# The first modulation vectors of a hybrid layer on TensorE: fp32 weights that stand still and a two-column vector that moves, with their first loads ahead of the token loads

## The chip, the cores and the metric

The kernel runs on one core of a Trainium2 chip. The metric is the device time of one execution in microseconds (us); lower is better. A core has five engines that each work through their own instructions in order: TensorE (PE in the profile, with its weight loads on a row of their own, PEld), VectorE (DVE), ScalarE (ACT), GpSimd (POOL) and SyncE (SP), which here issues nearly all of the DMAs.

## The reference, cut to what matters

One layer of a diffusion backbone: 512 latent tokens and 256 context tokens of width 1024. Two conditioning vectors, one for the latent tokens and one for the context, go through a matrix of 1024 x 6144 and give six modulation vectors each. The first two of the six (shift and scale) are applied to the normalised tokens ahead of one wide input projection:

```python
mod_x = (silu(c) @ w_ada + b_ada).reshape(1, 6, 1, 1024)
mod_c = (silu(c_ctx) @ w_ada + b_ada).reshape(6, 1024)
hc = rms_norm(ctx, norm1_w) * (1.0 + mod_c[1]) + mod_c[0]
hx = rms_norm(x, norm1_w) * (1.0 + mod_x[:, 1]) + mod_x[:, 0]
zs = hn @ w_in   # for hn = hc and hx: q, k, v and gates of two token mixers
```

Two recurrent mixers (a gated delta rule and an mLSTM), an output projection, a gated residual and a gated MLP with a 3x3 convolution follow. The output is compared in fp32, so the kernel keeps fp32 accuracy throughout.

## The kernel before

**Products.** A large product of fp32 accuracy is made as three products of a rounded type (fp32r): both operands are split into hi (a cast, ACT, line 104) and lo (fp32 minus hi, line 105, on DVE or POOL), and `mm3` (lines 112 to 116) adds hi*hi, hi*lo and lo*hi. In all of these the tokens are the moving operand and 128 columns of the weight matrix the standing one.

**First stage, about the first 80 us.** `streams` (line 345) loads six blocks of 128 tokens (two of context, four latent), squares and sums them on ACT (line 320), scales them (DVE, 322), turns them over on PE (327, eight transposes a block) and copies the turned halves to `xT` (ACT 330, DVE 332). Then a loop over k = 0 to 7 (128 channels each) needs the modulation of these channels: `stream_mod` makes hi of the modulated tokens on ACT (341: `hx` for the 512 latent tokens, `hc` for the 256 of the context), the fp32 value on DVE (342) and lo (343: DVE for `hx`, POOL for `hc`). The products of step k are 12 matmuls: the gates' 128 columns (`ps_gc`, `ps_gx`) and the first head's key columns (`pc_k`, `px_k`), three of 256 and three of 512 moving columns for each. Beside them the first head's query columns (`px_q`, weight `wq0`, 24 matmuls of 512 columns) are taken up as their operands come. When the loop has ended, ACT evicts the gates (411, 412), PE turns them (`ps_gt`, 441), DVE and ACT make the decays, PE forms the running sums (`ps_gs`, 456) and turns them again (`ps_gr`, 480), DVE copies them (482), a DMA writes them out (`gd`) and others read them back as the masks of all heads (`Eg`). The inverse of the delta rule's first heads starts from these masks.

**The modulation of the first stage** is 16 blocks of 1024 x 128 of `w_ada`, 512 KB each: `uw` k, j for channel block k and shift or scale j. `ada_load` (224) issues their DMAs on SP; the tiles share one tag of 7 buffers (`XN`) with the six token blocks and the assembled gate weights. `ada_rows` (231) lets the vectors stand and the weights move: for 14 blocks the weight is split into hi `uh` (ACT, 243) and lo `ul` (DVE or POOL, 244), and 16 matmuls run with 4 standing columns (hi and lo of both vectors, `sch`) and 128 moving (247); two blocks (`UF`) run as plain fp32 (239). The result is 4 rows of 256, which ACT copies (249); `ada_cols` (253) turns them with two small transposes (256) and DVE adds bias and parts (258, 261, 262) to give `mod` and `modA`.

**What sets the order.** A scheduler at build time lays out each engine's queue from the program order and its own model of durations; nothing moves at run time. An ACT instruction that waits for its operand holds all ACT instructions behind it, and the same goes for PE's matmuls. SP's DMAs of the first stage stand in the order tokens, first weights, `wk0`, the `uw` blocks, then `wq0` (`w_cols`, line 110, through `load_split`).

Of the kernel before, what the change touches and what calls it, by code (L numbers as in the profile page):

```python
# [70 lines left out]
class Kern:  # L71
# [131 lines left out]
    def ada_first(self, xp):  # L203
        nc, I, cp = self.nc, self.I, self.cp
        th = xp.tile([P, 16], F32, tag="c_th", name="c_th")
        nc.scalar.activation(th, self.ccol, AF.Tanh, scale=0.5)
        sc0 = xp.tile([P, 16], F32, tag="sc0", name="sc0")
        nc.vector.scalar_tensor_tensor(sc0, th, 1.0, self.ccol, ALU.add, ALU.mult)
        self.sc = cp.tile([P, KC, 2], F32, tag="sc", name="sc")
        nc.vector.tensor_scalar(self.sc.rearrange("p k j -> p j k"), sc0.rearrange("p (j k) -> p j k", j=2), 0.5, None, ALU.mult)  # L210
        self.sch = xp.tile([P, KC, 4], F32R, tag="sch", name="sch")
        nc.vector.tensor_copy(self.sch[:, :, 0:2], self.sc)
        nc.vector.tensor_tensor(self.sch[:, :, 2:4], self.sc, self.sch[:, :, 0:2].bitcast(F32), ALU.subtract)
        self.sc4 = xp.tile([P, KC, 4], F32, tag="sc4", name="sc4")
        nc.vector.memset(self.sc4, 0.0)
        nc.vector.tensor_copy(self.sc4[:, :, 0:2], self.sc)
        self.bada4 = xp.tile([P, 16, 4], F32, tag="bada4", name="bada4")
        nc.vector.memset(self.bada4, 0.0)
        nc.vector.tensor_copy(self.bada4[:, :, 0:2], self.bada[:, 0:16].unsqueeze(2).broadcast_to([P, 16, 2]))
        self.mod = cp.tile([P, 16, 2], F32, tag="mod", name="mod")  # L220
        self.modA = cp.tile([P, KC, 2], F32, tag="modA", name="modA")
        self.modB = self.mod[:, 0:8, :]

    def ada_load(self, k, j, xp):

        w = xp.tile([P, KC, P], F32, tag="xn", name=f"uw{k}_{j}", bufs=XN)
        c0 = D * j + P * k
        self.anchor["d"] = self.nc.sync.dma_start(w, self.I["w_ada"][0][:, c0 : c0 + P].rearrange("(k p) c -> p k c", p=P))
        return w

    def ada_rows(self, k, ap):

        nc = self.nc
        ps = self.pt([P, 512], ("mg", "po")[k % 2], f"ps_ada{k}")
        for j in range(2):
            w = self.uw[2 * k + j]
            if (2 * k + j) in UF:
                for i in range(KC):
                    nc.tensor.matmul(ps[0:4, P * j : P * j + P], self.sc4[:, i, :], w[:, i, :], start=i == 0, stop=i == KC - 1)
                continue  # L240
            hi = ap.tile([P, KC, P], F32R, tag="uh", name=f"uh{k}_{j}", bufs=UH)
            lo = ap.tile([P, KC, P], F32R, tag="ul", name=f"ul{k}_{j}", bufs=UH)
            nc.scalar.copy(hi, w)
            (nc.vector, nc.gpsimd)[(2 * k + j) in UP].tensor_tensor(lo, w, hi.bitcast(F32), ALU.subtract)
            for i in range(KC):
                for p in (hi, lo):
                    nc.tensor.matmul(ps[0:4, P * j : P * j + P], self.sch[:, i, :], p[:, i, :], start=i == 0 and p is hi, stop=i == KC - 1 and p is lo)
        r = ap.tile([4, 2 * P], F32, tag="adr", name=f"adr{k}", bufs=2)
        nc.scalar.copy(r, ps[0:4, 0 : 2 * P])
        return ps, r  # L250

    def ada_cols(self, k, ps, r, ap):

        nc = self.nc
        for j in range(2):
            nc.tensor.transpose(ps[:, 256 + 4 * j : 260 + 4 * j], r[:, P * j : P * j + P], self.ident[0:4, 0:4])
        t = ap.tile([P, 2, 4], F32, tag="adt", name=f"adt{k}", bufs=2)
        nc.vector.tensor_tensor(t, ps[:, 256:264].rearrange("p (n j) -> p n j", j=4),
                                self.bada4[:, k : 16 : KC, :], ALU.add)
# [74 lines left out]
    def stream_mod(self, k, xp):  # L334
        nc = self.nc
        A, B = self.modA[:, k, :], self.modB[:, k, :]
        for (h, n0, n1, j, e) in ((self.hx, NCTX, NALL, 0, nc.vector), (self.hc, 0, NCTX, 1, nc.gpsimd)):
            hh, hl = h
            src = self.xT[:, k, n0:n1]
            t = xp.tile([P, n1 - n0], F32, tag=f"hl_t{j}", name="hl_t", bufs=2 - j)  # L340
            nc.scalar.activation(hh[:, k, :], src, AF.Identity, bias=B[:, j : j + 1], scale=A[:, j : j + 1])
            nc.vector.tensor_scalar(t, src, A[:, j : j + 1], B[:, j : j + 1], ALU.mult, ALU.add)
            e.tensor_tensor(hl[:, k, :], t, hh[:, k, :].bitcast(F32), ALU.subtract)

    def streams(self):

        with self.tc.tile_pool(name="xin", bufs=1) as xp, self.tc.tile_pool(name="ada", bufs=2) as ap:
            self.xT = xp.tile([P, KC, NALL], F32, tag="xT", name="xT")
            self.vectors(xp, 0)
            xs = [self.stream_load(c, xp) for c in range(2)]  # L350
            self.vectors(xp, 1)
            xs += [self.stream_load(c, xp) for c in range(2, 6)]
            self.ada_first(xp)
            self.uw = [self.ada_load(n // 2, n % 2, xp) for n in range(2)]
            wg = self.gates_weights(xp)
            self.sub_eng = self.nc.gpsimd
            wk = self.w_cols(self.I["w_in"][0], 1024, "wk0")
            self.uw += [self.ada_load(n // 2, n % 2, xp) for n in range(2, 16)]
            for c in range(6):
                self.stream_in(c, xs[c], xp)  # L360
            gx, gc = (self.pt([P, 512], "prep", f"ps_{n}") for n in ("gx", "gc"))
            kc, kx = (self.pt([P, 512], "sc", n) for n in ("pc_k0", "px_k0"))
            a = self.ada_rows(0, ap)
            for k in range(KC):
                self.ada_cols(k, *a, ap)
                self.stream_mod(k, xp)
                if k < KC - 1:
                    a = self.ada_rows(k + 1, ap)
                for (w, pc, px) in ((wg, gc, gx), (wk, kc, kx)):
                    for (ps, h, n) in ((pc, self.hc, NCTX), (px, self.hx, NT)):  # L370
                        self.mm3(ps[:, :n], w[0][:, k, :], w[1][:, k, :], h[0][:, k, :], h[1][:, k, :], k == 0, k == KC - 1)
            self.gates_rows(gx, gc)
            self.first = {"wk": wk, "pc_k0": kc[:, :NCTX], "px_k0": kx}


    def gates_weights(self, xp):

        nc, I, cp, tc = self.nc, self.I, self.cp, self.tc
        w = I["w_in"][0]
# [1132 lines left out]
```

## Time and profile before

| what | value |
|---|---|
| time before, median of 3 runs | 1418.37 us (1417.46 to 1422.01) |
| the profiled execution | 1419.17 us, of which the span is 1417.5 us |
| PE busy | 1323.7 us, 93% of the span |
| DVE, ACT, POOL busy | 919.3, 588.7, 492.9 us |
| DMA | 141.86 MB, 100 GB/s over the span |

A profile's span runs from the first instruction to the last; the execution's own time is 1.7 us more. A line of the timeline gives start, duration, engine, line, operation and tiles, and in brackets how long the engine had been idle and what ended that. A window's row gives for each engine the busy time and the number of instructions in that stretch, the granted clock of PE (1.00 is full, 0.50 half), the DMA share and GB/s. A matmul's duration holds the time to get through the array, so the pace of back-to-back matmuls is read from their starts.

### The profile page before, as it was taken

To read this page: it belongs to the slowest core of one execution; us is meant where nothing else is said; L and a number is where in the kernel's file an instruction comes from. 1 tells how busy PE (TensorE), PEld (TensorE's weight loads), DVE (VectorE), ACT (ScalarE), POOL (GpSimd) and SP (SyncE) were. 2 spreads that over 40 slices of the span, in tenths; PEclk is the share of its full clock that TensorE was granted. 3 is DMA by queue.
4 is the path that set the end of the run, shared out by engine and by line. 5 is a ranking of instruction groups with operands and counts; after the bars stand their busy time and mean duration, and the time that the engine had idled before them with its cause. 6 is when DMAs were issued, how large, how long until landed. Compare 5 with 4: busy or idle time off the path is not lost.

```text
span 1417.5 us, 24242 instructions
## 1 busy us (share of the span) xinstructions
PE 1323.7 (93%) x9436; PEld 1118.2 (79%) x9436; DVE 919.3 (65%) x1900; ACT 588.7 (42%) x1283; POOL 492.9 (35%) x591
## 2 busy tenths in 40 slices
PE   5988699999999999999999999879989999999997
PEld 4777588878887887889788887668887888888886
DVE  6648973748676683554655367455469879879933
ACT  6555554545556554333333345112234333333331
POOL 4425131130330303242500004770145555555552
PEclk9999799999999999999999999999999999999999
DMA  8533233231332323343422214765523233333321
GB/s 244 151 87 94 56 80 85 72 101 42 84 81 67 79 53 88 107 132 111 113 62 76 64 45 111 185 173 172 189 67 112 86 93 105 89 105 89 104 89 60
DMA packets 233234, 141.86 MB, mean 100 GB/s; under 512 B 32978, under 2 KB 215519, under 8 KB 233119
## 3 DMA queue, kind: packets, MB, share of 16 engines
q1 hardware_dynamic: 233118, 140.31, 35.6%
q8 instruction: 74, 1.21, 0.4%
q14 instruction: 42, 0.34, 0.1%
HBM read 134.47 MB, written 5.82 MB: 99 GB/s over the span
## 4 chain that ended last, share of the span: by engine, by line
PE 60%; DMA 12%; POOL 9%; DVE 9%; ACT 5%; issue 3%; SPq 0%; POOLq 0%; DVEq 0%; ACTq 0%
PE pu L115 11%; PE pu L116 5%; PE pd L115 5%; PE px_g L115 3%; PE pv L115 3%; PE pd L116 3%; POOL iv_t L758 2%; POOL gx L760 2%; DMA scr<-cdx 2%; PE po L115 2%; PE px_mo L115 2%; DMA oTg<-in_w_ada_dram 2%; PE py L115 2%; PE px_g L116 2%; PE px_q L115 2%
## 5 line engine op out<-in xcount | busy, mean ns | idle before, releaser
L1482 DVE SCALAR_TENSOR_TENSOR y<-pu,fw,y 128x441 f32<-128x441 f32 (+2 forms) x352 | 229.9, 690 | 39.7 <-ACT y L1473 34.1
L1031 POOL TENSOR_TENSOR mkw<-mkt,colB 128x768 f32<-128x768 f32 x8 | 12.8, 1607 | 137.5 <-PE mpc L1052 79.3
L139 POOL TENSOR_TENSOR kh<-pw_t,phalf 128x6 f32<-128x6 f32 x8 | 11.1, 1390 | 124.1 <-DVE pw_t L138 124.1
L895 DVE SCALAR_TENSOR_TENSOR X<-p,colA,vt 128x128 f32<-128x128 f32 x80 | 24.2, 345 | 33.2 <-PE p L891 33.1
L275 POOL TENSOR_TENSOR oTg<-oTg,sc 128x512 f32<-128x512 f32 x22 | 34.5, 1576 | 29.4 <-DMA oTg<-in_w_ada_dram 29.0
L777 POOL TENSOR_TENSOR qs<-qs,qT 128x512 f32<-128x512 f32 x16 | 20.7, 1294 | 62.4 <-DMA qs<-gd 55.8
L139 POOL TENSOR_TENSOR rs<-pw_t,mhalf 128x1 f32<-128x1 f32 x14 | 9.1, 653 | 92.9 <-DVE pw_t L138 92.9
L753 POOL MEMSET gx<- 96x16 f32 x8 | 1.0, 124 | 115.3 <-DMA gx<-scr 115.3
L911 PE MATMUL p<-v,kt 128*128 128x128 f32 x160 | 30.2, 305 | 10.6 <-ACT v L907 10.6
L758 POOL TENSOR_TENSOR iv_t<-gx 96x14 f32<-96x14 f32 (+6 forms) x112 | 37.0, 330 | 7.5
L907 ACT ACTIVATE v<-p,sc 128x128 f32<-128x128 f32 x80 | 25.4, 367 | 34.0 <-PE p L899 33.8
L1473 ACT ACTIVATE y<-pu,fw 128x512 f32<-128x512 f32 x44 | 30.0, 683 | 20.5 <-PE pu L116 12.6
L760 POOL TENSOR_TENSOR gx<-gx,iv_t 96x14 f32<-96x14 f32 (+6 forms) x112 | 34.0, 304 | 8.7
L911 PEld LDWEIGHTS p<-v,kt 128*128 128x128 f32 x160 | 23.3, 197 | 16.7 <-ACT v L907 14.8
L626 DVE SCALAR_TENSOR_TENSOR Eg<-Eg,colA,mask 128x128 f32<-128x128 f32 x96 | 32.7, 405 | 3.9 <-DMA Eg<-gd 3.8
L1424 POOL TENSOR_TENSOR al<-y,ah 128x512 fp32r<-128x512 f32 x22 | 28.7, 1304 | 14.8 <-ACT ah L1423 11.7
L1056 DVE SCALAR_TENSOR_TENSOR C<-C,ge,mpc 128x257 f32<-128x257 f32 x32 | 15.4, 480 | 28.0 <-PE mpc L1052 27.8
L918 DVE SCALAR_TENSOR_TENSOR S<-S,ge,p 128x128 f32<-128x128 f32 x64 | 19.3, 343 | 18.4 <-PE p L911 17.3
L277 POOL TENSOR_TENSOR oTg<-oTg 128x256 f32<-128x256 f32 (+1 forms) x44 | 30.0, 699 | 0.7
L1434 DVE TENSOR_TENSOR fd_t<-pd,m 128x512 f32<-128x512 f32 x8 | 5.3, 684 | 37.8 <-PE pd L116 37.8
L891 PE MATMUL p<-S,kT 128*128 128x128 f32 x160 | 29.7, 287 | 0.0
L924 ACT ACTIVATE v<-p,sc 128x128 f32<-128x128 f32 x64 | 23.0, 378 | 15.8 <-PE p L911 15.0
(1239 smaller groups left out, 4683.9 us busy)
## 6 DMA issues: line engine op xcount, KB each, us to landing
uw<-in_w_ada_dram SPq DMA_DIRECT2D x16, 512.0 KB
oTg<-in_w_ada_dram SPq DMA_DIRECT2D x32, 256.0 KB
Eg<-gd SPq DMA_DIRECT2D x16, 384.0 KB
gx<-in_w_ada_dram SPq DMA_DIRECT2D x23, 256.0 KB
qs<-gd SPq DMA_DIRECT2D x16, 256.0 KB
aw<-in_w_ada_dram SPq DMA_DIRECT2D x9, 256.0 KB
xn<-in_x_dram SPq DMA_DIRECT2D x4, 512.0 KB
Em<-r1d SPq DMA_DIRECT2D x8, 256.0 KB
```

Of the source, the lines that this page charges most:

```text
L115: for i in (mm(out, lh, rh, start=start, stop=False), mm(out, lh, rl, start=False, stop=False), mm(out, ll, rh, start=False, stop=stop)):
L116: mm(out, ll, rh, start=False, stop=stop)):
L275: eng.tensor_tensor(w, w, self.sc[:, 4 * i : 4 * i + 4, 0:1].broadcast_to([P, 4, P]), ALU.mult)
L277: eng.tensor_tensor(w[:, 0:m, :], w[:, 0:m, :], w[:, m : 2 * m, :], ALU.add)
L626: self.follow(nc.vector.scalar_tensor_tensor(E[:, c, :], E[:, c, :], self.colA[:, c, d, row : row + 1], self.mask[d], ALU.add, ALU.min), "v")
L758: eng.tensor_tensor(t, Bi[:, 0:j, j : j + 1].broadcast_to([8 * NB, j, n]), Bi[:, j : j + 1, j + 1 :].broadcast_to([8 * NB, j, n]), ALU.mult)
L760: g = eng.tensor_tensor(Bi[:, 0:j, j + 1 :], Bi[:, 0:j, j + 1 :], t, ALU.add)
L891: g = nc.tensor.matmul(p1[:, d, :], kT[:, c * P : c * P + P], S[d], start=True, stop=True)
L911: g = nc.tensor.matmul(p3[:, d, :], kt[:, c, :], v3[d], start=True, stop=True)
L1424: nc.gpsimd.tensor_tensor(al[:, j, :], ys[0], ah[:, j, :].bitcast(F32), ALU.subtract)
L1473: nc.scalar.activation(y, ps, AF.Copy, scale=tap(0, 0))
L1482: g = nc.vector.scalar_tensor_tensor(o, u3[:, r0 + dy : r1 + dy, c0 + dx : c1 + dx], tap(dy, dx), o, ALU.mult, ALU.add)
```

## The change

The vectors no longer stand; the weights do. `ada_mod(k)` takes the fp32 block as it was loaded, as the standing operand of 128 x 128, and lets the two columns of `sc` move: 8 matmuls a block, which PE runs as two fp32 passes each. The result comes out with channels on partitions, so the split of the weights, the 4-row copy, the transposes, `sch`, `sc4` and `bada4` all go, and one DVE addition of the bias stands in their place. The shared tag has 12 buffers in place of 7. `uw` 0,0 and 0,1 are loaded ahead of the context, `uw` 1,0 and 1,1 ahead of x. `ada_mod(0)` is issued ahead of the token work and `ada_mod(k+1)` ahead of `stream_mod(k)`. The lo of `hc` moves from POOL to DVE. The small gate vectors (`gb`, `en`) are loaded after the `uw` blocks in program order, in a function of their own, `gates_vectors`, which holds what stood at the end of `gates_weights`.

```diff
-UH = 3
-UF = (1, 7)
-UP = (0, 9, 13)
-XN = 7
+XN = 12
...
-    def ada_rows(self, k, ap):
+    def ada_mod(self, k):
...
-        ps = self.pt([P, 512], ("mg", "po")[k % 2], f"ps_ada{k}")
+        ps = self.pt([P, 2, 2], ("mg", "po")[k % 2], f"ps_ada{k}")
         for j in range(2):
             w = self.uw[2 * k + j]
-            nc.scalar.copy(hi, w)
-            (nc.vector, nc.gpsimd)[(2 * k + j) in UP].tensor_tensor(lo, w, hi.bitcast(F32), ALU.subtract)
             for i in range(KC):
-                for p in (hi, lo):
-                    nc.tensor.matmul(ps[0:4, P * j : P * j + P], self.sch[:, i, :], p[:, i, :], start=i == 0 and p is hi, stop=i == KC - 1 and p is lo)
-        nc.scalar.copy(r, ps[0:4, 0 : 2 * P])
...
-    def ada_cols(self, k, ps, r, ap):
...
+                nc.tensor.matmul(ps[:, j, :], w[:, i, :], self.sc[:, i, :], start=i == 0, stop=i == KC - 1)
         m = self.mod[:, k : 16 : KC, :]
-        nc.vector.tensor_tensor(m, t[:, :, 0:2], t[:, :, 2:4], ALU.add)
+        nc.vector.tensor_tensor(m, ps, self.bada[:, k : 16 : KC].unsqueeze(2).broadcast_to([P, 2, 2]), ALU.add)
         nc.vector.tensor_scalar(self.modA[:, k, :], self.mod[:, KC + k, :], 1.0, self.n1w[:, k : k + 1], ALU.add, ALU.mult)
...
-        for (h, n0, n1, j, e) in ((self.hx, NCTX, NALL, 0, nc.vector), (self.hc, 0, NCTX, 1, nc.gpsimd)):
+        for (h, n0, n1, j, e) in ((self.hx, NCTX, NALL, 0, nc.vector), (self.hc, 0, NCTX, 1, nc.vector)):
...
             self.vectors(xp, 0)
+            self.uw = [self.ada_load(0, j, xp) for j in range(2)]
             xs = [self.stream_load(c, xp) for c in range(2)]
             self.vectors(xp, 1)
+            self.uw += [self.ada_load(1, j, xp) for j in range(2)]
             xs += [self.stream_load(c, xp) for c in range(2, 6)]
             self.ada_first(xp)
-            self.uw = [self.ada_load(n // 2, n % 2, xp) for n in range(2)]
             wg = self.gates_weights(xp)
             self.sub_eng = self.nc.gpsimd
             wk = self.w_cols(self.I["w_in"][0], 1024, "wk0")
-            self.uw += [self.ada_load(n // 2, n % 2, xp) for n in range(2, 16)]
+            self.uw += [self.ada_load(n // 2, n % 2, xp) for n in range(4, 16)]
+            self.gates_vectors()
+            self.ada_mod(0)
             for c in range(6):
                 self.stream_in(c, xs[c], xp)
...
-            a = self.ada_rows(0, ap)
             for k in range(KC):
-                self.ada_cols(k, *a, ap)
+                if k < KC - 1:
+                    self.ada_mod(k + 1)
                 self.stream_mod(k, xp)
-                if k < KC - 1:
-                    a = self.ada_rows(k + 1, ap)
```

The order of the instructions is the scheduler's, so three places of it are shown. Lines of the changed kernel are some 3 to 33 lower (341 is 308 there, 104 is 101, 115 is 112). The name in brackets is a semaphore waited for; DMAHW is a DMA's landing.

The first place is ACT in the channel loop. Before, the cast of the query weights (`wq0h`) stands behind four steps of `hx` and `hc`, and ahead of the other four:

```order
L341 ACTIVATE hx_75<-xT,mod,modA 128x512 [waits DVE_49]
L341 ACTIVATE hc_81<-xT,mod,modA 128x256
L243 CAST uh_0_751<-uw_0_240 128x1024 [waits DMAHW4_49,PE_49,Pool_49]
L249 COPY adr_653<-ps_ada_612 4x256 [waits PE_49]
L243 CAST uh_1_771<-uw_1_242 128x1024 [waits DMAHW5_49,PE_49,Activation_49]
L104 CAST wq0h<-wq0r 128x1024 [waits DMAHW0_49]
L243 CAST uh_0_820<-uw_0_244 128x1024 [waits DMAHW6_49,DVE_49,PE_49]
L249 COPY adr_722<-ps_ada_681 4x256 [waits PE_49]
L341 ACTIVATE hx_75<-xT,mod,modA 128x512 [waits DVE_49]
L341 ACTIVATE hc_81<-xT,mod,modA 128x256
L243 CAST uh_1_840<-uw_1_246 128x1024 [waits DMAHW7_49,PE_49,Activation_49]
```

In the changed kernel it stands right behind the last copy of the turned tokens:

```order
L297 COPY xT<-ps_xt_0_323 128x4x128 [waits PE_49]
L297 COPY xT<-ps_xt_0_343 128x4x128 [waits PE_49]
L308 ACTIVATE hc_81<-xT,mod,modA 128x256 [waits DVE_49]
L297 COPY xT<-ps_xt_0_363 128x4x128 [waits PE_49]
L101 CAST wq0h<-wq0r 128x1024 [waits DMAHW0_49]
L308 ACTIVATE hx_75<-xT,mod,modA 128x512 [waits Activation_49]
L308 ACTIVATE hx_75<-xT,mod,modA 128x512 x2
L308 ACTIVATE hx_75<-xT,mod,modA 128x512 [waits DVE_49]
L308 ACTIVATE hc_81<-xT,mod,modA 128x256
L308 ACTIVATE hx_75<-xT,mod,modA 128x512 [waits DVE_49]
```

What moved: with the 14 casts of `uw` gone, the cast of `wq0h`, which waits for a DMA, now stands ahead of every `hx`, from k = 0 on; only three of the `hc` are ahead of it.

The second place is PE in the channel loop. Before, the modulation of a later step (here `ps_ada` of k = 4) is spread among the products, and the rows of 4 x 128 are followed by a small transpose:

```order
L247 MATMUL ps_ada_612<-uh_0_613,sch 4x128
L247 MATMUL ps_ada_612<-ul_0_614,sch 4x128
L247 MATMUL ps_ada_612<-uh_0_613,sch 4x128
L247 MATMUL ps_ada_612<-ul_0_614,sch 4x128
L247 MATMUL ps_ada_612<-uh_0_613,sch 4x128
L247 MATMUL ps_ada_612<-ul_0_614,sch 4x128
L256 MATMUL ps_ada_555<-ident,adr_584 128x4 [waits Activation_49]
L256 MATMUL ps_ada_555<-ident,adr_584 128x4
L247 MATMUL ps_ada_612<-uh_1_633,sch 4x128
L115 MATMUL ps_gx<-hx_75,wgh 128x512 [waits Activation_49]
L115 MATMUL px_k_371<-hx_75,wk0h 128x512
L247 MATMUL ps_ada_612<-ul_1_634,sch 4x128 [waits Pool_49]
```

In the changed kernel each later step has one block of 16 matmuls of 128 x 2 (the block of k = 5 here; four rows stand for them) and then the 12 products of one k:

```order
L226 MATMUL ps_ada_535<-sc,uw_0_213 128x2 [waits DMAHW2_49,PE_49]
L226 MATMUL ps_ada_535<-sc,uw_0_213 128x2 x7
L226 MATMUL ps_ada_535<-sc,uw_1_215 128x2 [waits DMAHW3_49]
L226 MATMUL ps_ada_535<-sc,uw_1_215 128x2 x7
L112 MATMUL ps_gc<-hc_81,wgh 128x256 [waits Activation_49]
L112 MATMUL ps_gc<-hc_82,wgh 128x256 [waits DVE_49]
L113 MATMUL ps_gc<-hc_81,wgl 128x256
L112 MATMUL ps_gx<-hx_75,wgh 128x512
L112 MATMUL ps_gx<-hx_76,wgh 128x512
L113 MATMUL ps_gx<-hx_75,wgl 128x512
L112 MATMUL pc_k_377<-hc_81,wk0h 128x256
L112 MATMUL pc_k_377<-hc_82,wk0h 128x256
```

What moved: from k = 4 on, modulation and products alternate in whole blocks; the 24 products `px_q`, which before stood among them from k = 4 on, come around the products of k = 7, eleven of them ahead.

The third place is the head of SP's queue, before:

```order
L177 DMA rows<-in_c_dram 8x128
L177 DMA rows<-in_c_ctx_dram 8x128
L311 DMA xn_138<-in_ctx_dram 128x1024
L311 DMA xn_140<-in_ctx_dram 128x1024
L177 DMA rows<-in_norm_w_dram 8x128 x2
```

and in the changed kernel:

```order
L174 DMA rows<-in_c_dram 8x128
L174 DMA rows<-in_c_ctx_dram 8x128
L216 DMA uw_0_135<-in_w_ada_dram 128x8x128
L216 DMA uw_1_137<-in_w_ada_dram 128x8x128
L278 DMA xn_139<-in_ctx_dram 128x1024
L278 DMA xn_141<-in_ctx_dram 128x1024
```

What moved: 1 MB of `uw` stands ahead of the context. At the other end of the stage, all 16 `uw` stand ahead of `wq0r` in both.

More of the change, by code (lines that the diff above doesn't have):

```diff
@@ L210, in ada_first @@
         nc.vector.tensor_scalar(self.sc.rearrange("p k j -> p j k"), sc0.rearrange("p (j k) -> p j k", j=2), 0.5, None, ALU.mult)
[L211 to L219, printed above, removed]
         self.mod = cp.tile([P, 16, 2], F32, tag="mod", name="mod")
@@ L229, in ada_load @@
         return w
-    def ada_rows(self, k, ap):
+    def ada_mod(self, k):
         nc = self.nc
-        ps = self.pt([P, 512], ("mg", "po")[k % 2], f"ps_ada{k}")
+        ps = self.pt([P, 2, 2], ("mg", "po")[k % 2], f"ps_ada{k}")
         for j in range(2):
             w = self.uw[2 * k + j]
[L237 to L244, printed above, removed]
-            for i in range(KC):
-                for p in (hi, lo):
[L247 to L250, printed above, removed]
-    def ada_cols(self, k, ps, r, ap):
[L254 to L259, printed above, removed]
+            for i in range(KC):
+                nc.tensor.matmul(ps[:, j, :], w[:, i, :], self.sc[:, i, :], start=i == 0, stop=i == KC - 1)
         m = self.mod[:, k : 16 : KC, :]
-        nc.vector.tensor_tensor(m, t[:, :, 0:2], t[:, :, 2:4], ALU.add)
+        nc.vector.tensor_tensor(m, ps, self.bada[:, k : 16 : KC].unsqueeze(2).broadcast_to([P, 2, 2]), ALU.add)
         nc.vector.tensor_scalar(self.modA[:, k, :], self.mod[:, KC + k, :], 1.0, self.n1w[:, k : k + 1], ALU.add, ALU.mult)
@@ L345, in streams @@
     def streams(self):
-        with self.tc.tile_pool(name="xin", bufs=1) as xp, self.tc.tile_pool(name="ada", bufs=2) as ap:
+        with self.tc.tile_pool(name="xin", bufs=1) as xp:
             self.xT = xp.tile([P, KC, NALL], F32, tag="xT", name="xT")
             self.vectors(xp, 0)
+            self.uw = [self.ada_load(0, j, xp) for j in range(2)]
             xs = [self.stream_load(c, xp) for c in range(2)]
             self.vectors(xp, 1)
+            self.uw += [self.ada_load(1, j, xp) for j in range(2)]
             xs += [self.stream_load(c, xp) for c in range(2, 6)]
             self.ada_first(xp)
-            self.uw = [self.ada_load(n // 2, n % 2, xp) for n in range(2)]
             wg = self.gates_weights(xp)
@@ L391, in gates_weights, with gates_vectors @@
             nc.vector.tensor_copy(wg[:, :, 32 * d + 8 : 32 * d + 12], gi[:, :, 8 + 4 * d : 12 + 4 * d])
-        wgs = self.split(wg, [P, KC, P], "wg", xp)
+        return self.split(wg, [P, KC, P], "wg", xp)
+    def gates_vectors(self):
+        nc, I, cp = self.nc, self.I, self.cp
         gb = cp.tile([P, 1], F32, tag="gb", name="gb")
@@ L402, in gates_weights @@
         self.gb = gb
-        return wgs
     def gates_rows(self, psx, psc):
```

## The prediction

> **What bounds the kernel now.** Over the whole span PE is busy 93%, so I first looked for the stage in which the change lies, with the busy time of each engine in stretches of 8 us.
>
> ```profile
> core 0: us, PE busy (x) PEld busy (x) DVE busy (x) ACT busy (x) POOL busy (x), PEclk, DMA share, GB/s
> 16.00:24.00 8.00, 5.56 (x32) 4.54 (x30) 6.68 (x14) 4.59 (x9) 2.90 (x2) 0.71 0.71 177
> 32.00:40.00 8.00, 6.89 (x74) 5.67 (x74) 5.95 (x10) 3.85 (x7) 2.52 (x1) 1.00 1.16 291
> 48.00:56.00 8.00, 7.72 (x82) 6.41 (x81) 5.35 (x8) 5.38 (x8) 6.41 (x3) 1.00 0.60 154
> 64.00:72.00 8.00, 8.00 (x52) 6.73 (x52) 2.01 (x6) 1.67 (x3) 0.76 (x1) 1.00 0.00 0
> ```
>
> To about 50 us the stage follows its loads: the DMA share stands over 1 at 291 GB/s, and yet PE finds work for 6.9 and 7.7 of 8 us. From there to the end of the channel loop PE is the limit (8.00 of 8). The stage ends for the rest of the kernel when `ps_gt` runs. I then followed the chain of waits and the timelines from there.
>
> ```profile
> 78.96 0.88 PE L441 MATMUL ps_gt<-ident,oTg 128*128 128x128 f32 x6
> ```
> ```profile
> 96.56 0.42 DVE L482 COPY grr<-ps_gr 96x256 f32<-96x256 f32 x1 [5.73 <-PE ps_gr L480]
> 102.68 1.67 DVE L626 SCALAR_TENSOR_TENSOR Eg<-Eg,colA,mask 128x128 f32<-128x128 f32 x6 [2.40 <-DMA Eg<-gd]
> ```
> ```profile
> 156.00:160.00 4.00, 0.00 (x0) 0.00 (x0) 3.94 (x9) 0.75 (x3) 0.00 (x0) 0.50 0.00 0
> 160.00:164.00 4.00, 0.00 (x0) 0.00 (x0) 3.93 (x17) 0.86 (x2) 0.00 (x0) 0.50 0.00 0
> ```
>
> From `ps_gt` at 79.0 the gates' vectors go over small steps and two DMAs to the masks at 102.7, and further on PE itself stands still for 8 us (156 to 164) while DVE works off what began with these masks. So what moves `ps_gt` moves what follows, and PE's empty time there does not soak it up: DVE's work, for which it waits, comes later too. I take the shift of `ps_gt` as the shift of the end; up to 4 us may be given back where PE has other products to put ahead.
>
> **The change part by part.** *What goes.* These are the groups of the modulation on PE and ACT up to 80 us.
>
> ```profile
> L247 PE MATMUL ps_ada<-uh,sch 128*4 128x128 f32 x112 | 17.0, 235 | 0.0
> L247 PE MATMUL ps_ada<-ul,sch 128*4 128x128 f32 x112 | 16.8, 236 | 0.8 <-DVE ul L244 0.8
> L239 PE MATMUL ps_ada<-uw,sc 128*4 128x128 f32 x32 | 4.2, 291 | 0.0
> ```
> ```profile
> L243 ACT CAST uh<-uw 128x1024 fp32r<-128x1024 f32 x14 | 14.6, 1042 | 6.5 <-DMA uw<-in_w_ada_dram 5.4 <-ACT adr L249 0.7 <-PE ps_ada L247 0.3
> ```
> ```profile
> 48.71 0.22 PE L247 MATMUL ps_ada<-uh,sch 128*4 128x128 f32 x1
> 48.77 0.22 PE L247 MATMUL ps_ada<-ul,sch 128*4 128x128 f32 x1
> ```
>
> The starts are 0.06 us apart, so the 224 split matmuls hold PE for 13.4 us, and with 32 of line 239 and the transposes it is about 19 us. ACT loses 14.6 us of casts, DVE and POOL their lo parts. None of these engines was the one that all waited for ahead of 50 us; the loads were.
>
> *What comes on PE.* 16 blocks of 16 passes with a standing weight of 128 x 128 in fp32 and two moving columns, 256 in all. The nearest row is the running sums, with the same standing shape and 48 columns, at full clock.
>
> ```profile
> 84.53 1.96 PE L456 MATMUL ps_gs<-gu,gx 128*128 128x48 f32 x16 [0.53 <-PE pc_v L116]
> ```
> ```profile
> 84.50 1.86 PEld L456 LDWEIGHTS ps_gs<-gu,gx 128*128 128x128 f32 x16 [0.70 <-PE pc_v L116]
> ```
>
> Sixteen loads in 1.86 us are 0.116 us a pass, and the loads set the pace, so two columns cost what 48 do. 256 x 0.116 = 29.7 us: PE has some 10 us more to do than before, not less. Bounds: 0.06 us (line 247, if the load were hidden) and half clock, for which the loads of the `pad` matmuls, also 128 x 128 fp32, show 188 ns at the median and 335 at half clock, a factor of 1.78.
>
> ```profile
> L287 PEld LDWEIGHTS pad<-ones,oTg x32: 186/188/335, 892.2 to 969.9; 128*128 128x128 f32 x32
> ```
>
> *What moves on ACT.* This is the step that decides. Before, the cast of `wq0h` came when its weights did, with four steps of `hx` already made:
>
> ```profile
> 30.25 0.82 ACT L341 ACTIVATE hx<-xT,mod,modA 128x512 fp32r<-128x512 f32 x1
> 52.54 1.05 ACT L104 CAST wq0h<-wq0r 128x1024 fp32r<-128x1024 f32 x1 [0.84 <-DMA wq0r<-in_w_in_dram]
> ```
>
> Now it stands ahead of the first `hx`. Behind it in ACT's queue are all `hx`, five of the `hc`, and the gates' evictions; PE's next matmul waits for the first `hx`, DVE's lo for both. So the channel loop, which began at 30 us, begins when `wq0r` has landed. All 16 `uw` still stand ahead of it on SP. The DMA row up to 60 us (40 slices of 1.5 us) with its total says when that can be.
>
> ```profile
> GB/s 0 52 328 362 234 224 352 391 335 261 87 128 230 12 234 316 290 290 290 291 290 294 292 290 292 291 285 280 258 300 271 297 276 291 222 34 0 0 80 280
> DMA packets 24189, 14.00 MB, mean 233 GB/s; under 512 B 2774, under 2 KB 23415, under 8 KB 24183
> ```
>
> Of the 14.00 MB two blocks of 0.52 MB (`wv0r`, `wz0r`) come after, which leaves 12.95. The token blocks (3.1 MB) went at about 360 GB/s, the `uw` stream at 290: 2 + 8.7 + 33.8 = 44.5 us if no gap is left. The other bound is now's 52.5. More buffers close part of the gaps at 15 to 21 us, but SP now waits for landings of small loads (`gb`, `en`) between the `uw`, and the last `uw` need buffers that the last transposes free. I take 50.
>
> *The sum.* Cast 1.05, first `hx` 0.82: PE goes on at 51.9. What stands behind it up to `ps_gt`: 12 + 36 + 24 matmuls of 512 columns (`ps_gx` and `px_k` of k = 0 and 1, of the six other steps, `px_q`) and 36 of 256, and 128 passes of the modulation of k = 4 to 7. The pace at full clock and at half:
>
> ```profile
> 71.68 0.39 PE L115 MATMUL px_q<-hx,wq0h 128*128 128x512 f32 x1
> 71.91 0.39 PE L116 MATMUL px_q<-hx,wq0l 128*128 128x512 f32 x1
> 81.56 0.28 PE L116 MATMUL pc_v<-hc,wv0l 128*128 128x256 f32 x1
> 81.68 0.40 PE L115 MATMUL pc_v<-hc,wv0h 128*128 128x256 f32 x2
> 90.03 1.05 PE L115 MATMUL px_v<-hx,wv0h 128*128 128x512 f32 x2
> 90.89 0.63 PE L116 MATMUL px_v<-hx,wv0l 128*128 128x512 f32 x1
> 91.31 1.05 PE L115 MATMUL px_v<-hx,wv0h 128*128 128x512 f32 x2
> ```
>
> 512 columns take 0.23, 256 take 0.12; at half clock three of 512 take 1.28, 0.43 each, a factor of 1.85. 72 x 0.23 + 36 x 0.12 + 128 x 0.116 = 16.6 + 4.3 + 14.9 = 35.8 us. After a wait of some 10 us PE begins at half clock, which costs about 2.5. At full clock from then on `ps_gt` runs at 51.9 + 35.8 + 2.5 = 90.2, 11.2 later than 79.0.
>
> *The clock.* But the loop is now 3.7 us of standing weights (32 passes) and 2.1 us of products in turn, and what the gate grants is read from its own windows of 3.4 us.
>
> ```profile
> 83.99:87.40 3.41, 1.97 (x17) 1.86 (x16) 2.42 (x8) 2.48 (x5) 0.00 (x0) 1.00 0.64 167
> 87.40:90.82 3.42, 2.20 (x5) 1.82 (x6) 3.08 (x10) 1.83 (x6) 0.00 (x0) 0.50 0.02 5
> 493.58:496.99 3.41, 1.84 (x9) 1.33 (x9) 2.04 (x7) 3.19 (x9) 0.00 (x0) 1.00 0.00 0
> 496.99:500.41 3.42, 3.42 (x102) 2.67 (x105) 2.11 (x3) 1.64 (x2) 0.00 (x0) 1.00 0.00 0
> ```
>
> The window at 493.58 holds 1.84 us of wide matmuls and the next one is granted full clock. That at 83.99 holds 1.97 us, nearly all of it the 16 passes of `ps_gs`, and the next is at half. So a pass that waits for its load does not count as a busy PE does, and with two columns in place of 48 it counts less. A stretch of 3.7 us of such passes fills a whole window, so I expect half clock after the first (k = 4), and it comes back only after a window nearly full of wide products, which 2.1 us (3.9 at half) rarely give. That adds: three modulation stretches, 96 x 0.116 x 0.78 = 8.7; four steps of products, 4 x 2.1 x 0.85 = 7.1; one window at half in `px_q`, 1.6; less 2 for a step that finds the clock back: 15.4. `ps_gt` then runs at 105.6, 26.6 later.
>
> The Trainium skill, page "TensorE: Matmul & The Clock Gate", section "What's actually happening", has the clock fall after an idle window of about 3.4 us and rise after a busy one. By it, back-to-back passes would keep the clock and the time would be the first rival's, 1430.4; the row at 83.99, over half busy and followed by half clock, speaks against reading a load-bound pass as busy.
>
> **The rivals.** *The clock stays full.* If a standing pass counts as activity, only the late start is left: 1419.17 + 11.2 = 1430.4. For it: one window is thin evidence, and PE is never empty in the loop. Chance 0.27.
>
> *No change.* The loads of the weights hide (0.06 a pass, 128 x 0.056 = 7.2 us less than the sum) and `wq0r` lands near its lower bound (5 earlier): 11.2 - 12.2 = -1.0, 1418.2. Against it: the row of `ps_gs` has a pass at 0.116 with nothing else in the way. Chance 0.09.
>
> *Faster.* The wait for `wq0r` is short: with the loads ahead of the tokens and 12 buffers, the whole stream runs at the best slice of the DMA row, 391 GB/s, and lands at 2 + 12.95 / 0.391 = 35. PE goes on at 36.9, without a cold start, and `ps_gt` is at 72.7: 6.3 earlier, 1412.9. It decides from about 37 us downwards. Against it: 18 slices near 290 in a row at a DMA share of 1.16. Chance 0.07.
>
> That the change doesn't do what it says would need the fp32 passes to be other than two a matmul; line 239 already has 32 for 16, so I give it nothing of its own. Beyond all these, passes that cost more than the `ps_gs` row: 0.03.
>
> **How the numbers follow.** The sums are made against the profiled execution, 1419.17 us (0.06% over the median of 1418.37). The likeliest case, half clock in the loop (0.54), gives 1419.17 + 26.6 = 1445.8. The top of the range takes `wq0r` at 52.5 and the clock never back in the loop (+2.5, +2) with a little for the products after: 1453. The bottom, 1423, takes in the full clock with `wq0r` at 45 or 4 us given back, and leaves out the two cases that are not slower. A measurement of this kernel can tell 0.3%, 4.3 us, from no change: faster 0.07, same 0.09, slower 0.84.
>
> **What would show it.** Right: ACT idle at the cast of `wq0h` for some 5 us or more, ended by the DMA at about 50; no `hx` before 50; PE empty or nearly so ahead of it; 16 passes of line 226 in about 1.9 us at full and 3.3 at half clock; granted clock near 0.5 to 0.6 from 60 to 100; `ps_gt` at about 105; the same distance from `ps_gt` to the masks as before. Wrong: `hx` of k = 0 ahead of 40 us, or the clock at 1.0 through the loop (then 1430), or a shift of `ps_gt` that the end does not show.

## The result, and the profile after

The changed kernel takes 1438.53 us at the median of 4 runs (1433.15 to 1442.42), the kernel before 1418.08 (1417.46 to 1422.01). The ratio is 1.0129, 95% interval 1.0106 to 1.0152: slower by 1.3% (the two medians alone lie 20.4 us, 1.4%, apart). The forecast was 1445.8 us, with 1423 to 1453. The profiled execution took 1436.95 us (span 1435.2), 17.8 more than that of before, where the sum said 26.6.

The busy times of the first stage in stretches of 8 us, after the change:

```profile
core 0: us, PE busy (x) PEld busy (x) DVE busy (x) ACT busy (x) POOL busy (x), PEclk, DMA share, GB/s
...
16.00:24.00 8.00, 8.00 (x40) 8.00 (x39) 2.41 (x6) 5.07 (x9) 1.65 (x3) 1.00 0.94 287
...
32.00:40.00 8.00, 8.00 (x41) 8.00 (x41) 1.74 (x4) 1.62 (x3) 0.00 (x0) 1.00 0.96 263
...
48.00:56.00 8.00, 4.81 (x19) 4.00 (x19) 1.92 (x1) 3.17 (x4) 2.36 (x1) 1.00 0.69 167
...
72.00:80.00 8.00, 8.00 (x34) 7.63 (x35) 2.26 (x6) 1.31 (x2) 0.00 (x0) 0.50 0.00 0
80.00:88.00 8.00, 8.00 (x46) 7.34 (x45) 2.26 (x6) 1.31 (x2) 0.00 (x0) 0.71 0.01 2
```

PE is busy 8.00 of 8 us in the stretches from 16 to 24 and from 32 to 40 us, where it was busy 5.6 and 6.9 before. It has become the limit of a part of the stage that the loads had limited. The clock column has no event on record ahead of 61 us in this run and prints 1.00 there; the pace says otherwise. These are PE's rows of standing passes (`ps_ada`) and of transposes ahead of the loop, and where the loop begins:

```profile
13.24 1.97 PE L294 MATMUL ps_xt<-ident,xn 128*128 128x128 f32 x8 [1.46 <-DVE xn L289]
15.00 6.83 PE L226 MATMUL ps_ada<-sc,uw 128*128 128x2 f32 x32
21.69 1.95 PE L294 MATMUL ps_xt<-ident,xn 128*128 128x128 f32 x8
...
46.47 3.41 PE L226 MATMUL ps_ada<-sc,uw 128*128 128x2 f32 x16
...
54.10 0.80 PE L112 MATMUL ps_gx<-hx,wgh 128*128 128x512 f32 x1 [2.52 <-ACT hx L308]
...
56.37 0.79 PE L112 MATMUL ps_gx<-hx,wgh 128*128 128x512 f32 x1 [1.04 <-DVE hx L310]
```

And the blocks of 32 passes in the loop, with `ps_gt`:

```profile
63.57 3.63 PE L226 MATMUL ps_ada<-sc,uw 128*128 128x2 f32 x32
...
70.20 6.82 PE L226 MATMUL ps_ada<-sc,uw 128*128 128x2 f32 x32
...
80.87 4.04 PE L226 MATMUL ps_ada<-sc,uw 128*128 128x2 f32 x32
...
88.45 3.71 PE L226 MATMUL ps_ada<-sc,uw 128*128 128x2 f32 x32
...
103.54 0.82 PE L412 MATMUL ps_gt<-ident,oTg 128*128 128x128 f32 x6
```

Thirty-two passes took 6.83 us at 15 us and 3.63 at 63.6: 0.21 and 0.11 us a pass. The eight transposes ahead of the passes, at 13.2 us, took as long as the eight behind them (1.97 and 1.95 us). So PE ran at half clock from these transposes on until about 61, and in the loop the clock went up and down (blocks of 3.63, 6.82, 4.04 and 3.71 us). `ps_gt` comes at 103.5, 24.6 us later than before. On ACT:

```profile
45.11 0.59 ACT L297 COPY xT<-ps_xt 128x512 f32<-128x512 f32 x1 [1.81 <-PE ps_xt L294]
52.29 1.04 ACT L101 CAST wq0h<-wq0r 128x1024 fp32r<-128x1024 f32 x1 [6.59 <-DMA wq0r<-in_w_in_dram]
53.24 2.22 ACT L308 ACTIVATE hx<-xT,mod,modA 128x512 fp32r<-128x512 f32 x3
```

The cast of `wq0h` stands ahead of the first `hx` and waits 6.6 us for its load, as the order said. But PE's rows above show it empty for only 2.5 us ahead of 54.1 and 1.0 us ahead of 56.4: it was behind with its passes, and they covered most of the wait.

From `ps_gt` on, each span is split here at two more points: the first product of the merge of the two branches (`py`), and the last turn of the later modulation (`pad` from `ident`). For the profiled executions, in us:

| kernel | to `ps_gt` | to the merge | merge | rest | span |
|---|---|---|---|---|---|
| before | 79.0 | 786.0 | 110.7 | 441.8 | 1417.5 |
| changed | 103.5 | 784.9 | 105.2 | 441.6 | 1435.2 |

The first stage lost 24.6 us and the merge gave 5.5 back. The merge holds matmuls that wait for products which POOL, and once DVE, makes for the later modulation vectors (`pad`, line 287 before, 254 after). What PE waited for ahead of the `pad` matmuls of the merge, with the us and the number of waits, first before:

```profile
  POOL oTg L279: 10.4, 5
  DVE oTg L285: 2.1, 1
```

and after:

```profile
  POOL oTg L246: 6.7, 4
```

12.5 us against 6.7: the 5.8 us between them are about what the merge is shorter by. In the changed kernel these rows stand in another order among the products of the merge, though nothing of the merge was changed in the source.

### The profile page after: what moved, and what is told of

Same layout as the page of the kernel before. It is cut to its first block, busy times and chain, and to the rows that moved or that the text cites. A ratio compares the mean times of both kernels' runs of the same rounds, so it can differ in the third digit from the quotient of the medians.

```text
span 1435.2 us, 24134 instructions
## 1 busy us (share of the span) xinstructions
PE 1350.1 (94%) x9420; PEld 1152.1 (80%) x9420; DVE 911.9 (64%) x1883; ACT 573.2 (40%) x1261; POOL 477.3 (33%) x580
## 3 DMA queue, kind: packets, MB, share of 16 engines
HBM read 134.47 MB, written 5.82 MB: 98 GB/s over the span
## 4 chain that ended last, share of the span: by engine, by line
PE 62%; DMA 11%; DVE 10%; POOL 10%; ACT 4%; issue 3%; SPq 0%; POOLq 0%; DVEq 0%; ACTq 0%
PE pu L112 10%; PE pu L113 5%; PE pd L112 5%; PE px_g L112 3%; PE pv L112 3%; PE ps_ada L226 3%; PE pd L113 2%; POOL gx L731 2%; POOL iv_t L729 2%; DMA oTg<-in_w_ada_dram 2%; PE px_mo L112 2%; DMA scr<-cdx 2%; PE po L112 2%; PE px_g L113 2%; PE px_q L112 1%
## 5 line engine op out<-in xcount | busy, mean ns | idle before, releaser
L226 PEld LDWEIGHTS ps_ada<-sc,uw 128*128 128x128 f32 x256 | 48.0, 283 | 0.9
L226 PE MATMUL ps_ada<-sc,uw 128*128 128x2 f32 x256 | 45.3, 307 | 0.0
L731 POOL TENSOR_TENSOR gx<-gx,iv_t 96x14 f32<-96x14 f32 (+6 forms) x112 | 37.0, 330 | 8.6
L242 POOL TENSOR_TENSOR oTg<-oTg,sc 128x512 f32<-128x512 f32 x22 | 30.1, 1377 | 26.9 <-DMA oTg<-in_w_ada_dram 26.9
L878 ACT ACTIVATE v<-p,sc 128x128 f32<-128x128 f32 x80 | 25.4, 367 | 33.1 <-PE p L870 32.9
L882 PEld LDWEIGHTS p<-v,kt 128*128 128x128 f32 x160 | 22.8, 194 | 19.6 <-ACT v L878 17.8
L1027 DVE SCALAR_TENSOR_TENSOR C<-C,ge,mpc 128x257 f32<-128x257 f32 x32 | 15.4, 480 | 26.1 <-PE mpc L1023 26.0
L597 DVE SCALAR_TENSOR_TENSOR Eg<-Eg,colA,mask 128x128 f32<-128x128 f32 x96 | 28.6, 363 | 3.5 <-DMA Eg<-gd 3.5
```

The source lines that it names most:

```text
L226: nc.tensor.matmul(ps[:, j, :], w[:, i, :], self.sc[:, i, :], start=i == 0, stop=i == KC - 1)
L242: eng.tensor_tensor(w, w, self.sc[:, 4 * i : 4 * i + 4, 0:1].broadcast_to([P, 4, P]), ALU.mult)
L731: g = eng.tensor_tensor(Bi[:, 0:j, j + 1 :], Bi[:, 0:j, j + 1 :], t, ALU.add)
L882: g = nc.tensor.matmul(p3[:, d, :], kt[:, c, :], v3[d], start=True, stop=True)
```

## The experiments

**The cast out of the way.** The changed kernel with the cast of `wq0h` queued behind `hx` and `hc` of k = 3:

```diff
+        c = nc.scalar.copy(hi, raw)
+        if name == "wq0":
+            self.queue_after(c, self.hx_at)
...
+            if k == 3:
+                self.hx_at = g
```

> The changed kernel with one edge added: the cast of wq0h stands behind hx and hc of k = 3 on ACT, as it did before the change. Theory (half clock under standing passes is the larger part, the late start the smaller): PE was hardly ever empty ahead of 51 us, so only its 3.6 us of idle time between 51 and 56.4 go; ps_gt at about 100 in place of 103.5, time 3 to 5 us under the changed kernel (1433 to 1436). Rival (the late start is the cost, as the sum on record split it, 11 of 26 us): ps_gt at 92 to 95, time 9 to 12 us under it (1427 to 1430).

Measured: 1432.57 us (1430.80 to 1434.84), ratio to before 1.0110 [1.0087, 1.0134]; `ps_gt` at 102.1. The first three `hx` and the cast, and then the windows:

```profile
44.64 2.23 ACT L310 ACTIVATE hx<-xT,mod,modA 128x512 fp32r<-128x512 f32 x3
...
57.00 1.03 ACT L101 CAST wq0h<-wq0r 128x1024 fp32r<-128x1024 f32 x1
```
```profile
40.00:48.00 8.00, 8.00 (x41) 8.00 (x40) 5.18 (x11) 3.41 (x5) 0.00 (x0) 1.00 1.18 290
48.00:56.00 8.00, 8.00 (x33) 7.00 (x34) 1.30 (x4) 0.21 (x1) 0.00 (x0) 1.00 0.24 58
...
72.00:80.00 8.00, 8.00 (x37) 7.81 (x37) 0.44 (x3) 0.05 (x1) 0.00 (x0) 0.50 0.01 2
80.00:88.00 8.00, 8.00 (x34) 7.42 (x34) 1.82 (x4) 1.26 (x2) 0.00 (x0) 0.50 0.00 0
```

`hx` comes 8.6 us earlier and PE has no gap left, yet `ps_gt` gains only 1.4 us, since the loop is now at half clock for longer (0.50 from 72 to 88). The theory had expected 3.5 us at `ps_gt` and 3 to 5 in the time: the time, 6.0 us under the changed kernel (the two intervals overlap), lies just below its range, and the rival's 92 to 95 at `ps_gt` is far off. More of the time than of `ps_gt` moved; what gave the rest was not followed. With the passes at half clock, the late start is a small part of the cost.

**128 moving columns.** The same passes, with 126 columns of zeros added:

```diff
+        self.scw = xp.tile([P, KC, P], F32, tag="scw", name="scw")
+        nc.gpsimd.memset(self.scw, 0.0)
+        nc.vector.tensor_copy(self.scw[:, :, 0:2], self.sc)
...
-                nc.tensor.matmul(ps[:, j, :], w[:, i, :], self.sc[:, i, :], start=i == 0, stop=i == KC - 1)
+                nc.tensor.matmul(ps[:, j, :], w[:, i, :], self.scw[:, i, :], start=i == 0, stop=i == KC - 1)
```

> The changed kernel with 128 moving columns in place of 2 in the modulation (the two vectors and 126 columns of zeros; the first two columns of the result are used). With these costs the scheduler itself puts the cast of wq0h behind k = 3, so it is compared with the run that has only that. PE is given more to stream, the number of passes and loads stays 256. Theory (a load-bound pass doesn't count as activity, so the clock falls): a block of 32 passes takes 3.8 us everywhere, where the changed kernel shows 6.8 at half clock; the blocks and transposes ahead of 46 us shrink by 16 us, ps_gt at 76 to 82, time 1415 to 1422. Rival (passes cost what their loads cost and the clock has another reason, such as the transposes or waits): within 4 us of the run with the cast alone.

Measured: 1422.54 us (1419.55 to 1425.32), ratio 1.0039 [1.0025, 1.0054]; `ps_gt` at 76.1. PE's first block, the transposes behind it, a block of 22 passes, the blocks of the loop, and the windows:

```profile
13.85 5.07 PE L229 MATMUL ps_ada<-scw,uw 128*128 128x128 f32 x32
18.76 1.04 PE L297 MATMUL ps_xt<-ident,xn 128*128 128x128 f32 x8
19.63 2.62 PE L229 MATMUL ps_ada<-scw,uw 128*128 128x128 f32 x22
...
49.56 3.73 PE L229 MATMUL ps_ada<-scw,uw 128*128 128x128 f32 x32
...
56.90 3.73 PE L229 MATMUL ps_ada<-scw,uw 128*128 128x128 f32 x32
...
62.59 3.73 PE L229 MATMUL ps_ada<-scw,uw 128*128 128x128 f32 x32
...
76.07 0.82 PE L415 MATMUL ps_gt<-ident,oTg 128*128 128x128 f32 x6
```
```profile
32.00:40.00 8.00, 8.00 (x75) 8.00 (x73) 4.09 (x10) 3.90 (x6) 0.00 (x0) 1.00 1.16 291
40.00:48.00 8.00, 8.00 (x53) 7.25 (x52) 3.91 (x11) 1.36 (x3) 0.00 (x0) 1.00 1.16 290
...
56.00:64.00 8.00, 8.00 (x64) 7.60 (x63) 3.29 (x9) 1.76 (x3) 0.00 (x0) 1.00 0.15 44
64.00:72.00 8.00, 8.00 (x50) 7.10 (x50) 2.26 (x6) 1.31 (x2) 0.00 (x0) 1.00 0.00 0
```

There is more to stream, and blocks that took up to 6.8 us take 3.73, at a clock of 1.00; eight transposes take 1.04 us in place of 1.95. Against the run with the cast alone, `ps_gt` is 26.0 us earlier and the time 10.0 us less. The scheduler spread the passes otherwise here than in that run, but PE had no gap there and has the same matmuls to do ahead of `ps_gt` in both, so the 26 us are pace and not order. The clock is the cost of the first stage, and the rival falls. It is not all of the time: the kernel before took 1416.24 us beside these runs, so 10.0 of the 16.3 us between it and the run with the cast alone came back. The time, 1422.54, lies half a us above what was expected: `ps_gt` is 2.9 us earlier than in the kernel before, and the kernel is still slower than it. Where these 6.3 us arise is not settled; the profiled execution is the fastest of this kernel, 1419.55.

**48 and 24 columns.** Against the run with the cast alone only the width differs, and PE's order is the same up to the products of k = 7; with 128 columns the order is another (one execution each, so the times bear no interval).

> As the run with 128 moving columns, but with 48 (46 of them zeros), and the cast of wq0h held behind k = 3; only the width differs from that run and from the one with the cast alone. 48 is the width of ps_gs, whose window was followed by half clock. Theory (what counts is the time in which columns stream, about 0.045 of the 0.116 us of a pass, under half): blocks at half clock as with two columns, ps_gt at 95 to 103, time 1428 to 1436. Rival (any pass counts, and what kept the clock at two columns low was that next to nothing streams): full clock, ps_gt at 76 to 82, time 1417 to 1425.

> As the run with 48 moving columns, with 24. With 48 the clock did not rise while the passes ran alone with the transposes, but stayed full in the loop once it was there. Theory (a pass counts for its streaming columns and a little more, and the bound to keep the clock lies below that to regain it): at 24 columns the loop falls back to half clock as with 2, ps_gt at 97 to 103. Rival (what counts is that a pass runs at all, from a few columns on): the loop stays at full clock, ps_gt within 2 us of 87.8.

Measured: `ps_gt` at 87.8 with 48 columns and at 97.0 with 24 (times 1432.20 and 1420.68). With 48, the first block and the last in the loop:

```profile
13.97 6.90 PE L231 MATMUL ps_ada<-scw,uw 128*128 128x48 f32 x32
...
74.30 3.67 PE L231 MATMUL ps_ada<-scw,uw 128*128 128x48 f32 x32
```

With 24, the four blocks of the loop:

```profile
57.02 3.65 PE L231 MATMUL ps_ada<-scw,uw 128*128 128x24 f32 x32
...
62.70 3.76 PE L231 MATMUL ps_ada<-scw,uw 128*128 128x24 f32 x32
...
69.93 4.12 PE L231 MATMUL ps_ada<-scw,uw 128*128 128x24 f32 x32
...
77.86 6.86 PE L231 MATMUL ps_ada<-scw,uw 128*128 128x24 f32 x32
```

With 48 columns neither side was right: passes and transposes alone stay at half clock, but in the loop, where wide products had raised it, the clock holds. With 24 it gives way during the loop, as the theory had it. So the same passes, 48 columns wide, do not gain the clock at half and keep it at full. That need not mean two bounds. A pass takes 0.21 us at half clock and 0.11 at full (rows above), so 48 columns a pass are some 230 columns per us at half and 440 at full; 24 at full, which lose the clock, are 220, and 128 at half, which gain it, 610. One bound between 230 and 440 columns per us would give all four (an estimate from these rows, for passes alone). No run tells the two accounts apart.

The times run against `ps_gt`: with 24 columns it comes 9.2 us later than with 48, and that execution is 11.5 us shorter.

**The late start at full clock.** 128 columns, every `hx` held behind the cast, for which the load of `wq0` stands ahead of the loop in program order:

```diff
+            wq = self.w_cols(self.I["w_in"][0], 0, "wq0")
...
+            if j == 0 or k > 2:
+                self.queue_after(g, self.wq_at)
```

> 128 moving columns again, but the cast of wq0h is held ahead of every hx, as the scheduler had put it in the changed kernel. Against the changed kernel only the clock differs, against the other 128-column run only the late start. Theory: wq0r lands at about 50.4, PE goes on 1.9 us later with 35.8 us of work at full clock and some 2 us of half clock after its wait: ps_gt at 88 to 91, 12 to 15 us later than with the cast behind k = 3, and 60 to 100% of that at the end (time 1430 to 1437). Rival (the late start costs little, since it cost 4 to 6 us in the two-column kernel): time within 6 us of the other 128-column run (1419 to 1428).

Measured: 1426.83 us (1421.04 to 1427.46), ratio 1.0068 [1.0047, 1.0088]; `ps_gt` at 79.9, 3.8 us later than with the cast behind k = 3, and 4.3 us at the end. The theory falls, the rival holds:

```profile
38.83 8.87 PE L231 MATMUL ps_ada<-scw,uw 128*128 128x128 f32 x78
...
66.83 3.29 PE L231 MATMUL ps_ada<-scw,uw 128*128 128x128 f32 x28
```

78 passes of the modulation stand together at 38.8, ahead of the products, and fill the wait. The scheduler put them there in this version, so PE's order is not that of the changed kernel, and what the late start would cost at full clock with that order kept stays open. Behind the wait PE was at half clock again (granted 0.50 from 53 to 58 us), so not even this run is at full clock throughout. Against the changed kernel, with the cast in the same place, `ps_gt` goes from 103.5 to 79.9 and the median down by 11.7 us.

**The parts alone.** The standing weights in the kernel before (`ada_mod` in place of `ada_rows` and `ada_cols`, nothing else):

> The kernel before with one part of the change: the modulation by standing fp32 weights and two moving columns; loads, buffers (7), the gate vectors and the lo of hc stay as before. The scheduler puts the cast of wq0h behind five steps of hx. Theory (half clock under standing passes): blocks of 32 passes at 6.8 us for most of the stage, ps_gt at 95 to 102, time 1432 to 1440. Rival (the late start and the order of the loads are the cost): 1420 to 1427.

Measured: 1436.28 us (1434.45 to 1439.56), ratio 1.0138 [1.0113, 1.0163], `ps_gt` at 102.3, with the first `hx` at 29.5. It is as slow as the whole change, without the new loads and without an early cast: the theory holds, with `ps_gt` 0.3 us beyond its range. Of the six blocks of 32 passes in the loop the last three took 6.82 us, the others 3.7 to 4.1.

The loads (the first four `uw` ahead of context and x; the vectors stand, 7 buffers):

> The kernel before with the other part of the change: uw 0,0 and 0,1 are loaded ahead of the context and uw 1,0 and 1,1 ahead of x; the vectors stand as before, in 7 buffers. Theory (the loads' order is worth little, since PE is filled to about 50 us by what has landed and the stream's end stays): ps_gt within 3 us of 79.0, time within 4 us of 1418. Rival (the tokens come too late behind 2 MB of weights): ps_gt 4 to 8 us later, time 1422 to 1426.

Measured: 1412.74 us (1408.93 to 1414.61), ratio 0.9967 [0.9952, 0.9981], `ps_gt` at 79.9. The time lies 5.3 us under 1418, where the theory allowed 4, and 3.5 under the 1416.24 that the kernel before took beside it; the rival falls. It is faster than both kernels, but not by its first stage, which ends 0.9 us later than before. In its merge PE waits 4.5 us ahead of `pad` in place of 12.5:

```profile
  POOL oTg L279: 4.5, 3
```

The lo of `hc` on DVE, in the kernel before:

> The kernel before with the smallest part of the change alone: the lo of hc on DVE in place of POOL. Theory (POOL's wait of 25 us there was for ACT, not work that others waited for long): ps_gt within 2 us of 79.0 and the time within 4 us of 1417. The merge of the two branches, from 860 us on, is compared as well: if its length moves by several us here too, with the first stage unmoved, what it gives back in the changed kernel has nothing to do with the modulation. Rival: DVE, the busiest helper of the first stage, gets 8 x 0.4 us more and ps_gt comes 3 us or more later, 1420 to 1424.

Measured: 1414.18 us (1412.44 to 1421.86), ratio 0.9983 [0.9968, 0.9997]; `ps_gt` at 76.3, 2.7 us earlier, a little beyond what was allowed, and the merge at 109.9: it did not move with `ps_gt`. DVE's extra work cost nothing. Its profiled execution was the slowest of its runs, so its stages are not set against the median.

Both of the last two together:

> The kernel before with the two parts of the change that gained alone: the first uw ahead of the tokens, and the lo of hc on DVE; the vectors still stand. Theory (the gain of the first came in the merge, where PE waits 4.5 us for POOL's products in place of 12.7, and that of the second in the first stage, 2.7 us): if the order of the merge is kept, 1409 to 1413; if it falls back, 1413 to 1417. Rival (both gains were drawn by the scheduler's order and don't add): within 2 us of 1416.

Measured: 1417.15 us (1412.70 to 1421.26), ratio 1.0003 [0.9986, 1.0020], `ps_gt` at 81.1, the merge at 109.8. The two gains don't add, as the rival said; the theory's second case, a merge that falls back, gave 1413 to 1417 and is as near. The best kernel of this study is the one with the loads alone.

**All of them, split as above**, for the profiled executions, in us:

| kernel | to `ps_gt` | to the merge | merge | rest |
|---|---|---|---|---|
| cast later | 102.1 | 783.2 | 104.7 | 441.0 |
| standing alone | 102.3 | 783.0 | 109.0 | 440.2 |
| 24 columns | 97.0 | 780.4 | 102.0 | 439.5 |
| 48 columns | 87.8 | 793.7 | 108.3 | 440.7 |
| 128, late start | 79.9 | 794.8 | 109.9 | 441.2 |
| 128 columns | 76.1 | 793.1 | 108.3 | 440.4 |
| lo on DVE alone | 76.3 | 793.1 | 109.9 | 440.8 |
| loads alone | 79.9 | 789.9 | 101.2 | 440.9 |
| loads and lo | 81.1 | 787.1 | 109.8 | 440.7 |

Each row is one execution, up to 7.7 us from the median of its kernel, so a few us in a column show little. The rest hardly moves. The merge takes 101 to 105 us in four of the eleven kernels and 108 to 111 in the others, at an early `ps_gt` as at a late one. These four have the `pad` rows in one order among the products of the merge, and PE waits 4 to 7 us ahead of them; the other seven have another order, and PE waits 9 to 12.5 us. That the order is the reason is read from this, and no run changed it alone. The way to the merge is 780 to 785 us where `ps_gt` is late and 786 to 795 where it is early: part of an early `ps_gt` is lost again. On the average more than half of this arises in the next 100 us: the second turn of the gates' vectors (`ps_gt`, lines 562 and 533) comes 94 to 96 us behind the first in the four late kernels and 98 to 103 in the others. One piece of it can be seen. The masks (`Eg`, lines 626 and 597) are made on DVE in two lots of six, the second beside POOL's `qs`. Before, and then after:

```profile
102.68 1.67 DVE L626 SCALAR_TENSOR_TENSOR Eg<-Eg,colA,mask 128x128 f32<-128x128 f32 x6 [2.40 <-DMA Eg<-gd]
...
104.71 2.69 POOL L777 TENSOR_TENSOR qs<-qs,qT 128x512 f32<-128x512 f32 x2 [4.10 <-DMA qs<-gd]
...
104.86 5.82 DVE L626 SCALAR_TENSOR_TENSOR Eg<-Eg,colA,mask 128x128 f32<-128x128 f32 x6
...
107.36 2.39 POOL L105 TENSOR_TENSOR wq1l<-wq1r,wq1h 128x1024 fp32r<-128x1024 f32 x1
```
```profile
129.01 1.67 DVE L597 SCALAR_TENSOR_TENSOR Eg<-Eg,colA,mask 128x128 f32<-128x128 f32 x6 [2.02 <-DMA Eg<-gd]
...
130.99 1.66 DVE L597 SCALAR_TENSOR_TENSOR Eg<-Eg,colA,mask 128x128 f32<-128x128 f32 x6
131.12 4.21 POOL L748 TENSOR_TENSOR qs<-qs,qT 128x512 f32<-128x512 f32 x2 [5.41 <-DVE cv_y L548]
```

Before, POOL's two products began first, and DVE's six took 5.82 us where the first six had taken 1.67. After, DVE's six began 0.13 us ahead: they took 1.66, and POOL's two took 4.21 in place of 2.69. That is 4.2 us on the path of the masks, decided by a tenth. About half of it is lost again: two small steps of DVE behind the masks (lines 655 and 138 before, 626 and 135 after), still beside POOL's products, took 1.28 and 1.17 us after, where they had taken 0.17 and 0.13. In the other nine kernels the second lot falls the same two ways, drawn out where POOL had begun first (in three of them with another of its products) and not where DVE had. What else makes the stretch longer was not followed.

## Why the prediction was right, and where it was not

**The cast.** The mechanism was there: ACT stood for 6.6 us, the load landed at 52.3 (50 was taken), no `hx` came before 53. The size was wrong. The step "PE goes on at 51.9", with 11.2 us of loss, supposed a PE that stands empty; it was busy with passes at half clock, and taking the wait away brought 1.4 us at `ps_gt`. The sign "PE empty or nearly so ahead of it" failed with it.

**The clock.** The likeliest case was the right one, and its term too small: 15.4 us were set down, and the 128 columns took 26.0 off `ps_gt`. The half clock stood from PE's first transposes at 13 us, and the sum had no term for the stretch ahead of the loop. In the loop it was milder than reckoned: one of the three later blocks ran at half clock throughout, not three, since the products raised the clock again in between. The four blocks took 18.2 us, 3.7 more than four at 3.63, where the sum had 8.7 for three of them; and the clock column reads 0.75, 0.50, 0.71 and 0.75 from 64 to 96 us, where 0.5 to 0.6 was expected. A late start taken too large and a clock taken too small nearly cancelled, by luck: 105.6 forecast for `ps_gt`, 103.5 measured. The cause was named rightly and the total was good; its split was not.

The Trainium skill, page "TensorE: Matmul & The Clock Gate", section "What's actually happening", lets the clock rise after a busy window of about 3.4 us and fall after an idle one. Here PE had no idle window from 15 to 51 us and stayed at half clock, and columns of zeros brought the full clock back; for passes bound by their loads the runs go against it.

**The price of a pass.** Right: 0.116 us was taken, 0.113 measured at full clock (3.63 / 32) and 0.213 at half, a factor of 1.88 where 1.78 was taken.

**The shift of the end.** "I take the shift of `ps_gt` as the shift of the end; up to 4 us may be given back" failed in size: 24.6 us at `ps_gt` became 17.8 at the end, 5.5 of the difference in the merge, of which the prediction did not speak. This is most of the distance between 26.6 and 17.8; the other 2.1 is the earlier `ps_gt`. The widths of 24 and 48 columns show that the two need not even move the same way. The masks came 25.5 us behind `ps_gt`, where 23.7 was expected to stay.

**The rivals.** Full clock (1430.4): it fell with the rows of the loop, and with the run at 128 columns. No change, and faster: `wq0r` landed at 52.3 and a pass was not hidden, so neither had its condition.

**The range.** Its bottom, 1423, does not follow from the terms named for it: 1430.4 less 5 for `wq0r` at 45 us is 1425.4, less the 4 given back 1426.4, and less both 1421.4.

## What to carry to other kernels

A matmul with a wide standing operand and a handful of moving columns costs its weight load, and a long run of them leaves TensorE at half clock, for the products and transposes among them too: before a product is turned that way round, ask whether the array would stream or only load. A wait on one engine is not yet a loss; look at what the engine behind it still has to do, and at its pace, before the wait goes into the sum. Where a scheduler lays out the whole program, order in a stage that nobody touched can move by 5 to 10 us (the merge took 101.2 to 110.7 here), so split the span into stages before a cause is named.

## What the runs showed of the hardware that was not expected

Adding work can pay: 126 columns of zeros a pass took 26.0 us off the first stage. The same passes can run at either clock: with 48 columns they stayed at half clock where they began at it (6.90 us a block), and at full clock where wide products had raised it (3.67); a memory of the gate would do this, and so would one bound on the columns streamed per us. And DVE and POOL hold each other up: where the masks met POOL's products, the one that had begun first went on at its own pace (DVE 1.66 us, POOL 2.69), and the other was drawn out (DVE to 5.82, POOL to 4.21).
